# A hybrid decoder block on one core: where the rotated q/k projections stand among the plain ones, and who orders the second half of the projections

## The chip, the cores and the metric

The kernel runs on one core of a Trainium2 chip. The metric is the device time of one execution in microseconds, the median of the runs; lower is better. The engines are named as the profile names them: PE (TensorE matmuls) and PEld (its weight loads), DVE (VectorE), ACT (ScalarE), POOL (GpSimd) and SP (SyncE, which here only issues DMAs). Each engine works through its own instructions in a fixed order, and waits on semaphores where it needs another engine or a DMA.

## The reference, cut to what matters

One layer of a decoder block over 2048 positions of width 1024, all in float32:

```python
h = rms_norm(x, g_norm) * (1.0 + scale) + shift
proj = h @ w_in          # 1024 -> 8 x 1024
x_rnn, z_rnn, q, k, v, z_attn, g_r, g_a = split(proj)
# branch A: conv, gates, scan over x_rnn; times silu(z_rnn); @ w_out_rnn
# branch B: q and k get a partial rotary turn, then dilated attention
qh = apply_partial_rope(q.reshape(B, S, N_HEADS, HEAD_DIM), cos, sin)
kh = apply_partial_rope(k.reshape(B, S, N_HEADS, HEAD_DIM), cos, sin)
```

The rotary turn touches the first 32 of the 128 channels of each of the 8 heads: `x1*cos - x2*sin` and `x2*cos + x1*sin`, with `x1` and `x2` 16 channels each. The other 96 channels of q and k pass unturned. After the two branches come their output projections, sigmoid merge gates, one more projection and a final norm.

## The kernel before

**The stages.** Sequence positions are cut into four banks of 512 columns, and two banks make a half. For each half `f` in (0, 1) the kernel projects v first (`values_half`, which also builds the operands of the second bank), then the other seven blocks of `w_in` as 28 *pairs* (a pair is 256 output rows by the half's 1024 columns), and at the end comes a long stage that weaves attention with the output projections. In the trace the pairs of the first half run from about 150 to 752 us, those of the second from about 849 to 1445 us, and the last stage from there on.

**A pair** (`strassen`, L349) multiplies a 2x2 block of the weights with a 2x2 block of the activations by Winograd's scheme, in seven *products*. A product is 12 matmuls (four k-blocks, each float32 value as a high and a low part, three matmuls for a product of two such numbers). The products accumulate in the PSUM tiles X (two buffers), Z, W, V and Y (one each). ACT copies X to `u1`, DVE makes `u2` from Z and `u3` from W, and four *totals* leave a pair through `done(i, j, ps, u)`: after products V (1,1), X (0,0) and Y (1,0), and after the last product V (0,1), which is issued one product into the next pair (`last_product`, L409). So between the end of a pair's last V and the next pair's first V on the same PSUM tile there stand two products, Z and W; in that time DVE must have read the total.

**Who prepares the weight operands.** In the first half each product's weight operand `S` is made on the way: SP loads raw blocks `R` (256 KB, L254), DVE forms Winograd sums `s` (L285, L286, L294, L299), ACT rounds to the high part (L159), POOL subtracts for the low part (L165), and ACT's queue stores the result (512 KB, L277) to DRAM as `sD`. In the second half SP loads the finished `S` from `sD` (L318), seven tiles ahead, one each time a product is done with its tile. Instead, the second half prepares the output projections' weights (`output_weights`, L421): 32 blocks, every six products one, each a load `R` (L430) at product 6x+1, one ACT and one POOL operation at 6x+4 into the single-buffered tiles `s1` and `s2`, and two 256 KB stores `wD` (L440) at 6x+6.

**The order.** A counter `n_prod` counts products. `steps_after` and `later` put a step after a given product: when that product has been traced, `run_late` (L219) traces the steps that are due. Within `tc.manual_schedule()` each engine gets its instructions in the order in which the program traces them. Outside it, the framework's scheduler orders them with the help of a simulated time line, and may pull a later instruction ahead. Before the change the first half's pairs stand in such a block (L1202 to L1204), and the second half's don't.

**The pairs of a half** (`pair_order`, L1057, and the loop at L1206): 22 pairs (recurrent, gate and two plain q ones) from the pool `rp`, then the *tail* of six pairs from the pool `qp`: q rotated, k rotated, and four plain ones (q, k, k, k). A rotated pair (L996) holds the 32 turned channels of all 8 heads. Each of its totals takes a tile `t0`; q is scaled by ACT first (L988 or L993); then a step `shuffle` (DVE stream shuffle into `t1`, L1007, and POOL's `t0*Ct`, L1008), and one product later a step `add` (DVE's `t1*St`, L1012, and `t1+t0`, L1013) with four stores. `t0` has 4 buffers in the first half and 5 in the second, `t1` has 3. A plain pair (L1034) has the totals, for q the scaling, and stores.

**What else is in the tails.** In the first half's tail `next_norm` (L1147) loads the next bank of x (two loads of 1 MB on SP at once, L501), squares it on ACT with row sums (L1154, steps 5 to 8), takes the inverse root (steps 9 and 10) and scales it on DVE (L1158, steps 11, 13, 15, 17). During the last pair `next_even` (L1163) turns it on PE (L521) and builds eight operand parts (`build`, L524: ACT L531, DVE `hf` L538, then DVE L168 or POOL L165). In the second half's tail `residual_gate` (L1113) loads eight 512 KB blocks `gw` and adds them up on DVE (L1126, L1128), one every third product.

Of the kernel before, what the change touches and what calls it, by code (L numbers as in the profile page):

```python
# [10 lines left out]
F32 = mybir.dt.float32  # L11
# [9 lines left out]
P = 128  # L21
S = 2048
D = 1024
# [66 lines left out]
def decoder_block(ctx, tc, x, c, positions, g_norm, w_mod, b_mod, w_in, b_gate, conv_w, conv_b,  # L90
# [422 lines left out]
    n_built = [0]  # L513

# [8 lines left out]

    def build(st, names, xs, k, first=False, keep=None, pt=None):  # L524

        hh, hl = B[names[k // KH]]
        if pt is None:
            pt = turned(xs, k)
        pv = pt[:].rearrange("p r j -> p (r j)")
        g, s = gs[:, k : k + 1], sh[:, k : k + 1]  # L530
        nc.scalar.activation(hh[:, k % KH, :], pv, AF.Identity, bias=s, scale=g)  # L531
        if keep is not None or first:
            hf = keep if keep is not None else T(st, [P, CH], F32, "hf", bufs=2)[:]
            last_copy[0] = nc.scalar.activation(hf, pv, AF.Identity, bias=s, scale=g).ins
            last_lo[0] = lo_dve(hl[:, k % KH, :], hf, hh[:, k % KH, :])
        else:
            hf = T(st, [P, CH], F32, "hf", bufs=2)
            nc.vector.tensor_scalar(hf[:], pv, g, s, ALU.mult, ALU.add)  # L538
            (lo_dve if k % 3 == 0 else lo_pool)(hl[:, k % KH, :], hf[:], hh[:, k % KH, :])
# [442 lines left out]
    NT0, NT1 = (4, 5), 3  # L982
# [13 lines left out]
    def rotated_pairs(qp, f, Ct, St):  # L996

        for base, dstT, qs in QK:
            def rotated(i, j, ps, u, dstT=dstT, qs=qs):
                n = 2 * f + j  # L1000
                cq = slice(j * CH, (j + 1) * CH)
                t0 = T(qp, [P, CH], F32, "t0", bufs=NT0[f])
                wait, v = scaled(t0, ps, u, qs), []

# [4 lines left out]

                def add():  # L1010
                    t1 = v[0]
                    nc.vector.tensor_tensor(t1[:], t1[:], St[:, cq], ALU.mult)  # L1012
                    nc.vector.tensor_tensor(t1[:], t1[:], t0[:], ALU.add)  # L1013
# [40 lines left out]
    others = [1, 2, 2, 1, 2, 2, 1, 3]  # L1054
    is_plain = lambda n: n % 6 == 3

    def pair_order():  # L1057
# [89 lines left out]
    def next_norm():  # L1147

        xs = load_x(xp, 2, "x", 2)
        ss = T(xp, [P, 3, 4], F32, "ss")  # L1150

        def square(r):
            jk = T(xp, [P, D], BF16, "hf", bufs=2)
            nc.scalar.activation(jk[:], xs[r], AF.Square, accum_out=ss[:, 0, r : r + 1])  # L1154

        for r in range(4):
            later(5 + r, lambda r=r: square(r))
            later(11 + 2 * r, lambda r=r: nc.vector.tensor_scalar(xs[r], xs[r], ss[:, 1, r : r + 1], None, ALU.mult))  # L1158
        later(9, lambda: rstd_first(ss))
        later(10, lambda: rstd_last(ss))  # L1160
# [22 lines left out]
    for f in range(2):  # L1183
# [18 lines left out]
        if f == 0:  # L1202

            order.enter_context(tc.manual_schedule())  # L1204
# [11 lines left out]
        plain_at[0] = lambda: T(qp, [P, CH], F32, "t0", bufs=NT0[f])  # L1216

        touch = [T(qp, [P, CH], F32, tag, bufs=n) for tag, n in (("t0", NT0[f]), ("t1", NT1), ("u1", 1), ("u2", 2), ("u3", 1))]
# [584 lines left out]
```

## Time and profile before

| what | value |
|---|---|
| median of the runs | 2324.31 us (2319.95 to 2330.45) |
| span of the profiled execution, first to last instruction | 2322.0 us |
| median less that span | 2.3 us |
| PE busy | 2233.7 us (96%), 11459 matmuls |
| DVE, ACT, POOL busy | 1347.5, 1238.5, 971.1 us |
| moved by DMA | 573.41 MB, 247 GB/s over the span |

The profile gives the profiled execution's span and no time of its own beside it; what lies around the span is taken as the 2.3 us between it and the median. Three views are used below. The table by stage has, for each stretch of time, its length, then the busy time of PE, PEld, DVE, ACT and POOL with the number of instructions in brackets, the share of full TensorE clock that was granted, the mean busy share of the DMA engines, and GB/s. The table of waits has who waited for whom: microseconds in total, times, the longest. The timeline has start, duration, engine, line, operation, output<-input, and in square brackets how long the engine had been idle and what ended that. In the groups of instructions the number after the bar is busy time, then the mean ns of one, then idle time before them. Matmul ends are modelled, so starts are the better guide on PE.

### The profile page before, as it was taken

The numbers are of one execution on the slowest core, as the hardware profiler recorded it, in microseconds if no ns is written. First come the engines' busy times: TensorE is split into PE (matmuls) and PEld (weight loads), VectorE is DVE, ScalarE is ACT, GpSimd is POOL, SyncE is SP. The second block draws the span as 40 slices with busy tenths as digits, with TensorE's granted clock in tenths as the row PEclk, the third lists the DMA queues.
The fourth block names the chain that finished last, engine by engine and source line by source line (L and its number), as shares of the span: only waits on it lengthen the run. The fifth ranks groups of instructions, "written<-read, shape, count | busy, mean of one in ns | idle before, by whom it ended". The sixth has DMA issues, their size and how long they took to land.

```text
span 2322.0 us, 34101 instructions
## 1 busy us (share of the span) xinstructions
PE 2233.7 (96%) x11459; PEld 1868.9 (80%) x11461; DVE 1347.5 (58%) x2424; ACT 1238.5 (53%) x2412; POOL 971.1 (42%) x734
## 2 busy tenths in 40 slices
PE   8999999999979998999999999999989898989998
PEld 4998788888858997877888877888879797868887
DVE  4828787768483706344444362367666777667343
ACT  4737667668433625555546311567768777534211
POOL 1457576766465333323111020446565655433100
PEclk9999999999989999999999999999999999999999
DMA  7367787887989487998776897979988888798532
GB/s 262 105 216 246 248 290 252 291 282 256 295 253 299 125 266 269 318 312 283 247 227 201 280 290 234 294 245 270 274 252 253 240 249 243 232 313 276 170 123 95
DMA packets 429013, 573.41 MB, mean 247 GB/s; under 512 B 72135, under 2 KB 293027, under 8 KB 427813
## 3 DMA queue, kind: packets, MB, share of 16 engines
q1 hardware_dynamic: 390996, 451.47, 63.3%
q10 hardware_dynamic: 37648, 119.70, 13.3%
q8 instruction: 91, 1.49, 0.3%
q14 instruction: 86, 0.70, 0.1%
q0 software_dynamic: 192, 0.05, 0.0%
HBM read 357.18 MB, written 213.91 MB: 246 GB/s over the span
## 4 chain that ended last, share of the span: by engine, by line
PE 50%; DMA 9%; DVE 4%; ACT 3%; issue 2%; POOL 1%; SPq 1%; ACTq 0%; DVEq 0%; POOLq 0%
PE pj L151 11%; PE pq L151 8%; PE X L151 7%; PE V L151 7%; PE o L151 3%; PE Y L151 3%; PE sc L151 3%; PE Z L151 3%; PE W L151 3%; DMA R<-yaT 1%; DMA vraw<-vN 1%; DMA R<-oT 1%; PE pT L1419 1%; PE pg L151 1%; DMA wD<-s 1%
## 5 line engine op out<-in xcount | busy, mean ns | idle before, releaser
L151 PE MATMUL pj<-yh,S 128*128 128x512 f32 x1024 | 369.1, 405 | 5.5 <-DMA S<-wD 4.2
L151 PE MATMUL V<-T,S 128*128 128x512 f32 x1344 | 338.7, 401 | 22.6 <-DVE t L451 9.6
L151 PE MATMUL X<-T,S 128*128 128x512 f32 x1344 | 332.5, 396 | 3.9 <-ACT u L384 3.9
L165 POOL TENSOR_TENSOR S<-R,S 128x512 fp32r<-128x512 f32 x168 | 251.9, 1510 | 181.2 <-ACT S L159 66.0
L151 PEld LDWEIGHTS V<-T,S 128*128 128x128 f32 x1344 | 257.6, 193 | 86.5 <-ACT S L159 7.9
L151 PEld LDWEIGHTS X<-T,S 128*128 128x128 f32 x1344 | 253.8, 189 | 64.4 <-ACT u L384 4.4
L151 PEld LDWEIGHTS pj<-yh,S 128*128 128x128 f32 x1024 | 194.2, 190 | 42.8 <-DVE fg L1626 4.6
L151 PE MATMUL pj<-yl,S 128*128 128x512 f32 x512 | 202.0, 395 | 0.0
L1335 ACT ACTIVATE pp<-pp,st 128x256 f32<-128x256 f32 (+3 forms) x256 | 134.0, 524 | 107.1 <-DVE st L1334 106.3
L165 POOL TENSOR_TENSOR S<-s,S 128x512 fp32r<-128x512 f32 x84 | 129.0, 1536 | 136.4 <-ACT S L159 94.6
L151 PE MATMUL W<-T,S 128*128 128x512 f32 x672 | 167.2, 397 | 0.4 <-POOL S L165 0.4
L151 PE MATMUL Z<-T,S 128*128 128x512 f32 x672 | 165.7, 395 | 0.0
L151 PE MATMUL Y<-T,S 128*128 128x512 f32 x672 | 165.4, 395 | 0.0
L151 PEld LDWEIGHTS W<-T,S 128*128 128x128 f32 x672 | 126.9, 190 | 30.8 <-issue 0.9
L151 PEld LDWEIGHTS Y<-T,S 128*128 128x128 f32 x672 | 126.7, 189 | 29.5
L151 PEld LDWEIGHTS Z<-T,S 128*128 128x128 f32 x672 | 126.3, 188 | 29.3
L168 DVE TENSOR_TENSOR ptl<-pT,pth 128x384 fp32r<-128x384 f32 (+1 forms) x160 | 97.9, 629 | 64.6 <-ACT pth L159 62.3
L159 ACT ACTIVATE S<-R 128x512 fp32r<-128x512 f32 x168 | 102.1, 622 | 48.8 <-DMA R<-in_w_in_dram 17.7
L829 DVE SCALAR_TENSOR_TENSOR xc<-xr,par,xc 128x512 f32<-128x512 f32 x96 | 93.2, 971 | 57.6 <-ACT xc L823 56.0
L1399 ACT ACTIVATE pp<-pp,M 128x256 f32<-128x256 f32 (+3 forms) x256 | 118.0, 523 | 9.0 <-DVE M L1523 9.0
L1334 DVE CUSTOM_DVE_ANT_0 pp<-sc,msk 128x256 f32<-128x256 f32 (+3 forms) x256 | 105.1, 449 | 26.0 <-PE sc L151 23.4
L165 POOL TENSOR_TENSOR vh<-vraw,vh 128x256 fp32r<-128x256 f32 (+1 forms) x64 | 67.2, 1049 | 103.5 <-ACT vh L159 91.6
(327 smaller groups left out, 4708.9 us busy)
## 6 DMA issues: line engine op xcount, KB each, us to landing
sD<-S ACTq DMA_DIRECT2D x196, 512.0 KB, 4.0
S<-sD SPq DMA_DIRECT2D x196, 512.0 KB, 5.3
S<-wD SPq DMA_DIRECT2D x99, 512.0 KB, 5.5
R<-in_w_in_dram SPq DMA_DIRECT2D x136, 256.0 KB, 4.0
wD<-s ACTq DMA_DIRECT2D x64, 256.0 KB, 5.4
T<-in_w_mod_dram SPq DMA_DIRECT2D x8, 1024.0 KB, 12.0
vN<-ev SPq DMA_DIRECT2D x64, 128.0 KB, 2.8
zaT<-ev SPq DMA_DIRECT2D x32, 256.0 KB, 3.2
```

The costliest lines, as they stand in the source:

```text
L151: last_mm[0] = nc.tensor.matmul(o, lhsT=l, rhs=r, start=st, stop=sp, **kw).ins
L159: nc.scalar.activation(o, i, AF.Copy)
L165: nc.gpsimd.tensor_tensor(o, i, h.bitcast(F32), ALU.subtract)
L168: return nc.vector.tensor_tensor(o, i, h.bitcast(F32), ALU.subtract).ins
L829: nc.vector.scalar_tensor_tensor(xc, xr[:, i : i + CH], cw(i), xc, ALU.mult, ALU.add)
L1334: nc.vector.tensor_tensor_reduce(pdst, s_ps, mask, 1.0, 3e38, ALU.add, ALU.min, m_)
L1335: nc.scalar.activation(pdst, pdst, AF.Exp, bias=m_, scale=-1.0, accum_out=l_)
L1399: nc.scalar.activation(pp, pp, AF.Copy, scale=w)
L1419: nc.tensor.transpose(pt[:, c0 + j * P : c0 + (j + 1) * P], pp[i][:, k * P : (k + 1) * P], ident)
```

## The change

- `TAIL_ROTATED = (0, 1, 0, 1, 0, 0)`: the tail's order is now plain q, rotated q, plain k, rotated k, plain k, plain k, in both halves; `rotated_pairs` becomes a generator to be taken one at a time.
- A rotated total goes in three steps instead of two, each one product after the one before: shuffle (with POOL's product), turn (DVE's `t1*St`), add (DVE's sum, and the stores). The second total of a pair starts a product later than it did, and the third and fourth two products later.
- `t0` has 5 buffers in both halves. For the first half's tail pool `xp`, `hf` has one buffer instead of two.
- `next_norm` issues its two loads of x after products 3 and 10, squares at 16, 18, 20 and 22, takes the root at 23 and 25 and scales at 26, 28, 30 and 32.
- The second half's pairs stand in `tc.manual_schedule()` as well.

```diff
+    def n_hf(st):
+        return 1 if st is xp else 2
 ...
-            hf = T(st, [P, CH], F32, "hf", bufs=2)
+            hf = T(st, [P, CH], F32, "hf", bufs=n_hf(st))
 ...
-    NT0, NT1 = (4, 5), 3
+    NT0, NT1 = 5, 3
 ...
                 wait, v = scaled(t0, ps, u, qs), []
+                wait += (0, 1, 2, 2)[made[0]]
+                made[0] += 1
 ...
+                def turn():
+                    nc.vector.tensor_tensor(v[0][:], v[0][:], St[:, cq], ALU.mult)
+
                 def add():
                     t1 = v[0]
-                    nc.vector.tensor_tensor(t1[:], t1[:], St[:, cq], ALU.mult)
                     nc.vector.tensor_tensor(t1[:], t1[:], t0[:], ALU.add)
 ...
-                steps_after(n_prod[0], ((wait, shuffle), (wait + 1, add)))
+                steps_after(n_prod[0], ((wait, shuffle), (wait + 1, turn), (wait + 2, add)))
 
             strassen(qp, f, (base, "rotated"), rotated)
+            yield
 ...
+    TAIL_ROTATED = (0, 1, 0, 1, 0, 0)
 ...
-        for base, _, _ in QK:
-            yield (base, "rotated"), [wcol(base + hh * P, 32) for hh in range(H)]
-        for key in plain:
-            yield key, plain_pieces(*key)
+        rotated = iter(QK)
+        for r in TAIL_ROTATED:
+            if r:
+                base = next(rotated)[0]
+                yield (base, "rotated"), [wcol(base + hh * P, 32) for hh in range(H)]
+            else:
+                key = next(plain)
+                yield key, plain_pieces(*key)
 ...
-        xs = load_x(xp, 2, "x", 2)
+        xs = []
         ss = T(xp, [P, 3, 4], F32, "ss")
 
+        def load(r):
+            t = T(xp, [P, 2, D], F32, "x", bufs=2)
+            nc.sync.dma_start(t[:], xv[2, r : r + 2].rearrange("r j d -> j r d"))
+            xs.extend((t[:, 0, :], t[:, 1, :]))
 ...
+        later(3, lambda: load(0))
+        later(10, lambda: load(2))
         for r in range(4):
-            later(5 + r, lambda r=r: square(r))
-            later(11 + 2 * r, lambda r=r: nc.vector.tensor_scalar(xs[r], xs[r], ss[:, 1, r : r + 1], None, ALU.mult))
-        later(9, lambda: rstd_first(ss))
-        later(10, lambda: rstd_last(ss))
+            later(16 + 2 * r, lambda r=r: square(r))
+            later(26 + 2 * r, lambda r=r: nc.vector.tensor_scalar(xs[r], xs[r], ss[:, 1, r : r + 1], None, ALU.mult))
+        later(23, lambda: rstd_first(ss))
+        later(25, lambda: rstd_last(ss))
 ...
         order = ExitStack()
-        if f == 0:
-
-            order.enter_context(tc.manual_schedule())
+        order.enter_context(tc.manual_schedule())
 ...
-        rotated_pairs(qp, f, *tabs)
-        for n, _ in enumerate(plain, 3):
-            if n == 5 and f == 0:
+        rotated = rotated_pairs(qp, f, *tabs)
+        for n, r in enumerate(TAIL_ROTATED):
+            if n == len(TAIL_ROTATED) - 1 and f == 0:
                 next_even()
+            next(rotated if r else plain)
```

More of the change, by code (lines that the diff above doesn't have):

```diff
@@ L532, in build @@
         if keep is not None or first:
-            hf = keep if keep is not None else T(st, [P, CH], F32, "hf", bufs=2)[:]
+            hf = keep if keep is not None else T(st, [P, CH], F32, "hf", bufs=n_hf(st))[:]
             last_copy[0] = nc.scalar.activation(hf, pv, AF.Identity, bias=s, scale=g).ins
@@ L1215, in decoder_block @@
         plain_pool[0] = qp
[L1216 to L1218 removed]
+        plain_at[0] = lambda: T(qp, [P, CH], F32, "t0", bufs=NT0)
+        touch = [T(qp, [P, CH], F32, tag, bufs=n) for tag, n in (("t0", NT0), ("t1", NT1), ("u1", 1), ("u2", 2), ("u3", 1))]
         tabs = load_tables(qp, f)
```

8 lines of the change are left out of this document (5 added, 3 removed).

## The prediction

> **What bounds the kernel now.** I read the head of the page first, then a table by stage, then TensorE's waits in each stage, and for the long waits the timeline.
>
> ```profile
> span 2322.0 us, 34101 instructions
> PE 2233.7 (96%) x11459; PEld 1868.9 (80%) x11461; DVE 1347.5 (58%) x2424; ACT 1238.5 (53%) x2412; POOL 971.1 (42%) x734
> ```
>
> PE is busy 96% of the span. So an order of issue can win only what PE loses by waiting, and by the slower clock after a long wait. Cutting the trace where the stages begin shows where that is (columns: length, busy PE, PEld, DVE, ACT, POOL, clock, DMA share, GB/s):
>
> ```profile
> 150.60:609.40 458.80, 453.21 (x1950) 366.19 (x1949) 345.03 (x372) 316.83 (x505) 311.19 (x210) 1.00 0.78 267
> 609.40:750.00 140.60, 125.57 (x538) 100.88 (x538) 75.36 (x101) 45.71 (x81) 77.96 (x55) 0.94 0.88 281
> 849.40:1317.80 468.40, 457.12 (x1950) 368.35 (x1949) 211.74 (x285) 252.51 (x382) 108.52 (x85) 0.99 0.80 269
> 1317.80:1444.60 126.80, 124.29 (x521) 98.04 (x519) 53.92 (x73) 16.35 (x28) 16.89 (x12) 0.99 0.86 275
> ```
>
> These are the first half's 22 pairs, its tail, the second half's 22 pairs, and its tail. A product at full pace is this row of the chain:
>
> ```profile
> 682.23 2.79 PE X L151 x12
> ```
>
> 2.79/12 = 0.2325 us a matmul. The 22 pairs are 154 products and 96 gate matmuls, 1944 x 0.2325 = 452.0 us, with some 1.4 us of small transposes 453.4 us. The first half needs 458.8 for them and loses **5 to 6 us**; the second needs 468.4 and loses **15**. A tail's stretch holds 42 to 43 products, about 119 us, plus 2 to 3 us of transposes, first matmuls of the next stage or gate sums: the first tail loses **19 us**, the second **5**. Together about 45 us can be won in the stages that the change touches, and the rest of the span is not touched. The waits, first tail, then the second half's pairs, then its tail (total, times, longest):
>
> ```profile
> PE V L151 <- ACT S L159: 7.5, 1, 7.5
> PE V L151 <- DVE t L451: 7.2, 2, 7.0
> ...
> PE V L151 <- DVE ev L451: 3.8, 1, 3.8
> PE pg L948 <- DVE ev L943: 3.7, 1, 3.7
> PE pg L151 <- POOL xl L165: 2.9, 2, 1.4
> ...
> PE V L151 <- DVE t L451: 2.4, 1, 2.4
> ```
>
> So the first tail has two holes of 7 us, the second half a handful of small ones. The first hole in the timeline:
>
> ```profile
> 621.85 3.41 SPq L501 DMA_DIRECT2D x<-in_x_dram  x2
> ...
> 634.68 1.06 ACT L1154 ACTIVATE hf<-x 128x1024 bf16<-128x1024 f32 x1 [6.86 <-DMA sD<-S]
> ...
> 635.74 0.62 ACT L993 ACTIVATE t<-t 128x512 f32<-128x512 f32 x1
> ...
> 636.40 0.73 DVE L1007 STREAM_SHUFFLE t<-t 128x512 f32<-128x512 f32 x1
> ...
> 647.11 0.68 DVE L451 TENSOR_TENSOR t<-V,u 128x512 f32<-128x512 f32 x1
> ...
> 647.94 4.44 PE L151 MATMUL V<-T,S 128*128 128x512 f32 x12 [7.01 <-DVE t L451]
> ```
>
> Both loads of x are issued at 621.9, and land 12.8 us after issue:
>
> ```profile
> x<-in_x_dram SPq DMA_DIRECT2D x2, 1024.0 KB, 12.8
> ```
>
> 621.9 + 12.8 = 634.7, which is when ACT starts the first square after 6.9 us of idling (the row names a store; the landing fits better). Behind the square stands the scaling of q (L993), behind that DVE's shuffle, and behind the whole rotation the total that PE's V waits for. The second hole:
>
> ```profile
> 674.56 1.74 DVE L299 TENSOR_TENSOR s<-R,s 128x512 f32<-128x512 f32 x1
> ...
> 676.38 0.63 ACT L159 ACTIVATE S<-s 128x512 fp32r<-128x512 f32 x1 [10.14 <-DVE s L299]
> ...
> 677.05 5.18 PE L151 MATMUL V<-T,S 128*128 128x512 f32 x12 [7.50 <-ACT S L159]
> ```
>
> Here ACT waits 10.1 us for a Winograd sum, which stands in DVE's order behind rotations and scalings of x. DVE is simply late.
>
> **The change part by part.** *x in two parts, squares later.* The second load comes after product 10 and the first square after 16: 6 x 2.79 = 16.7 us, against a landing of 12.8 for both at once. SP's raw loads for the rotated pair no longer stand behind 2 MB. The first hole goes, 7.0 us and the slow product after it (4.3 instead of 2.79, from the starts 647.94 and 652.21): 8.5 us. If the cover fails, ACT stands as before, but in a plain pair.
>
> *Rotations apart, in three steps.* The groups of the first tail, and L1013 of the second tail, where POOL is nearly idle:
>
> ```profile
> L165 POOL TENSOR_TENSOR S<-R,S 128x512 fp32r<-128x512 f32 x29 | 41.3, 1431 | 20.3 <-ACT S L159 9.7 <-DMA R<-in_w_in_dram 7.5 <-issue 3.0
> L1012 DVE TENSOR_TENSOR t<-t,St 128x512 f32<-128x512 f32 x8 | 12.5, 1558 | 0.0
> L1013 DVE TENSOR_TENSOR t<-t,t 128x512 f32<-128x512 f32 x8 | 10.9, 1362 | 0.8
> L1158 DVE TENSOR_SCALAR x<-x,ss 128x1024 f32<-128x1024 f32 x4 | 4.2, 1038 | 0.0
> ...
> L1013 DVE TENSOR_TENSOR t<-t,t 128x512 f32<-128x512 f32 x8 | 5.4, 680 | 0.2
> ```
>
> With the shuffle's 0.73 (timeline above) a rotation costs DVE 1.56 + 1.36 + 0.73 = 3.65 us beside POOL's work. Two pairs in succession are 14 products, 39.1 us. Before, the two rotated pairs ask DVE for 8 rotations (29.2), 10 sums and totals from PSUM at 0.68 (6.8), 8 Winograd sums at no less (5.4) and four scalings of 1.04 (4.2): 45.6 us, **6.5 more than there is**, about the second hole. After, a rotated pair with the plain one behind it asks 14.6 + 6.8 + 5.4 = 26.8, with the x scalings 31.0, of 39.1. So the second hole goes too (7.5, and 5.02 - 2.79 = 2.2 for the slow product). POOL's 14 splits at 1.43 and four products fit as well (26 of 39.1). The third step itself adds nothing but waiting time for the tile, and the fifth `t0` covers it. What is late next is the start of the tail, where DVE idles for the gate stores of the pool before:
>
> ```profile
> 625.04 0.69 DVE L385 TENSOR_TENSOR u<-Z,u 128x512 f32<-128x512 f32 x1 [9.48 <-DMA gaT<-ev]
> ```
>
> A plain pair absorbs these 9.5 us: DVE has 9 x 0.68 = 6 us to do in its 19.5. Of 19 us I take **17**, since both holes lose their cause; bounds 8.5 (only the first hole) and 19.
>
> The Trainium skill ("SBUF — State Buffer", Who interferes with whom) says that a DVE instruction with two SBUF inputs and a GpSimd instruction reading SBUF exclude each other for a whole instruction. The trace goes part of the way: 0.68 alone, 1.36 to 1.56 beside POOL, not 0.68 + 1.3. Taken strictly, the rule lets me add both engines up: 18 POOL operations at 1.29 and 20 DVE ones at 0.69 make 37 of 39.1 us behind the rotated k, a margin of 2 us instead of 8. That speaks for the second rival below.
>
> *One `hf`.* DVE's next `hf` must wait for POOL's use of the last:
>
> ```profile
> L538 DVE TENSOR_SCALAR hf<-pg,gs,mod 128x512 f32<-128x512 f32 x6 | 4.8, 808 | 4.9 <-ACT T L531 4.9
> ...
> L165 POOL TENSOR_TENSOR T<-hf,T 128x512 fp32r<-128x512 f32 x3 | 3.9, 1294 | 4.2 <-DVE hf L538 4.2
> ```
>
> 0.81 + 1.29 = 2.1 us a build, in series. One build a product (2.79) hides that; the last three stand in a row and cost up to 3 x 0.81 = 2.4 us more, partly beside v matmuls that are ready. Queued behind the waiting `hf` are totals, which have two products to spare. I take **+1**; bounds 0, and 8 x 1.43 = 11 if every build waits for a split of the next stage's weights on POOL.
>
> *Second half, 22 pairs, program order.* The nearest evidence is the first half: the same pairs in the same order in such a block, 458.8 instead of 468.4 us, though DVE is busy 345 us there instead of 212, ACT 317 instead of 253 and POOL 311 instead of 109 (stage table). Its one long wait:
>
> ```profile
> PE X L151 <- ACT u L384: 3.9, 1, 3.9
> 263.28 1.28 ACT L936 ACT_TABLE_LOAD   x1
> ...
> 270.53 0.57 ACT L384 ACTIVATE u<-X 128x512 f32<-128x512 f32 x1
> ```
>
> That `u` stands behind table loads for the sines and, among others, three or four weight splits of 0.62 us, which the second half doesn't have. So the stage should come out between 458.8 (-9.6) and 453.4 (-15). I take the middle, **-12**. The output weights' steps move with it: the scheduler had pulled them to the front, into the busiest DMA stretch, with a quiet one behind it:
>
> ```profile
> 849.40:1105.00 255.60, 243.39 (x1022) 194.55 (x1021) 0.98 0.88 301
> 1105.00:1317.80 212.80, 212.41 (x914) 171.70 (x913) 1.00 0.71 230
> L440 ACTq DMA_DIRECT2D wD<-s x58: 326/326/627, 850.6 to 1076.8; - x58
> R<-in_w_out_attn_dram SPq DMA_DIRECT2D x16, 256.0 KB, 5.9
> ```
>
> 58 of the 64 stores stand before 1076.8; now they spread over 192 products. 32 x 768 KB = 25 MB over 595 us are 42 GB/s on top of 230: a share of 0.71 x 272/230 = 0.84 instead of 0.88 and 0.71. Tiles `S` are asked for 6 x 2.79 = 16.7 us ahead. SP now issues each of them after the product that frees its tile and before that product's stores, which costs a store no more than the product.
>
> *Second tail.* The same spreading of rotations removes the 2.4 us wait and its slow product, but weights traffic is added to a share of 0.86 (stage table): 0.86 x 317/275 = 0.99. I take **-2**, nearer to the first; bounds -4 and +8 (42 GB/s too much for 24 products, paid in full).
>
> *Into attention.* Two ordered blocks now follow each other; what lies between them (rounding `yh`, `yl`) is still free. **0**; bounds 0 and +6, were ACT's eight roundings to start behind the half's last total.
>
> Sum: 2322.0 - 17 + 1 - 12 - 2 = 2292 us span; with 2.3 us around it **2294.3 us** against the median of 2324.3. 0.5%, about what a measurement of this kernel can tell from no change, is 11.6 us: up to 2312.7 counts as faster.
>
> **The rivals.** *The second half gains nothing*: program order swaps the scheduler's holes for its own, because the output weights now sit among the recurrent steps to the end. For it: ACT and POOL wait on `wD` there already. Against: the first half with 7 more ACT operations a pair. 2322.0 - 17 + 1 + 2.3 = **2308**.
>
> *The rotated k stays too much for DVE and POOL*: its scalings of x (products 26 to 32) fall on its rotations, and the second hole remains. 2294.3 + 9.7 = **2304**.
>
> *Slower, by late output weights*: in program order ACT reaches the split of block x three products after SP issued its load, 8.4 us. If it lands later, ACT stands, and behind it `u`, the sigmoids, q's scaling; then DVE, then PE. The load takes 5.9 us now (row above), at a similar share. Before, ACT waited on these tiles too, and the stage lost 15 us:
>
> ```profile
> L159 ACT ACTIVATE s<-R 128x512 fp32r<-128x512 f32 x29 | 18.1, 626 | 36.8 <-DMA wD<-s 30.2 <-POOL s L165 3.1 <-DMA R<-in_w_out_rnn_dram 3.0
> ```
>
> 36.8 us of ACT's waiting with at most 15 us of PE's loss: 0.4 of it at worst. A landing of 13 us would be 32 x 4.6 = 147 us of waiting and 60 us lost: 2294 + 60 = **2354**. It decides from 30/0.4/32 = 2.3 us over 8.4, a landing of 10.7, on.
>
> **How the numbers follow.** Forecast 0.60, nothing from the second half 0.14, rotated k 0.12, late weights 0.14. The range takes in the first three: low end 2322 - 19 - 15 - 4 + 2.3 = 2286, less some us of scatter, 2281; high end 2308 with `hf` at its worse bound, 2318. Faster: 0.60 + 0.12 and somewhat under half of 0.14 (2308 is near the bound), 0.78; same 0.08; slower 0.14.
>
> **What would show it.** In the tail after: x landed before ACT's first square, no idling of ACT ahead of it, no wait of PE over 2 us; rotations at 3 us or more apart. In the second half: the 22 pairs in 455 to 459 us, `wD` stores out to the end of the tail, and a share near 0.84 in its middle. The forecast is wrong if PE waits for DVE or ACT in most second-half pairs, or if ACT's waits on `s` grow past 70 us.

## The result, and the profile after

| kernel | median | range | profiled execution | its span |
|---|---|---|---|---|
| before, in the same series | 2322.13 us | 2319.84 to 2330.45 | | 2322.0 us |
| after | 2298.52 us | 2293.75 to 2299.88 | 2299.88 us | 2298.1 us |

The ratio is **0.9889** (95% interval 0.9869 to 0.991): 1.1% faster, 4 us above the forecast of 2294.3. That the total came out near the forecast says little about its terms, as the stage table shows. The head of the page after:

```profile
span 2298.1 us, 34088 instructions
PE 2231.0 (97%) x11461; PEld 1867.5 (81%) x11461; DVE 1352.7 (59%) x2424; ACT 1239.5 (54%) x2412; POOL 974.6 (42%) x734
```

PE has the same work as before (2233.7 us busy then) in a span that is 24 us shorter. The table by stage, columns as before: the first half's 22 pairs, its tail, the projection of v, the second half's 22 pairs, its tail. A stage begins where its first product starts, and the tails end at the start of the last V.

```profile
150.56:609.35 458.79, 453.21 (x1951) 366.23 (x1949) 345.09 (x372) 316.78 (x505) 311.29 (x210) 1.00 0.77 268
609.35:743.42 134.07, 125.44 (x544) 100.97 (x543) 78.41 (x99) 46.33 (x81) 79.53 (x55) 0.97 0.94 290
743.42:840.26 96.84, 96.84 (x808) 96.27 (x807) 51.32 (x84) 47.29 (x84) 37.55 (x27) 1.00 0.47 142
840.26:1290.89 450.63, 450.63 (x1950) 365.36 (x1949) 209.11 (x285) 251.05 (x378) 105.50 (x81) 1.00 0.83 272
1290.89:1410.74 119.85, 119.81 (x509) 94.78 (x508) 48.69 (x72) 16.58 (x28) 22.44 (x16) 1.00 0.98 320
```

Of before, the stretch of v, and the second tail with its end cut in the same way (the others are in the prediction):

```profile
750.04:849.41 99.37, 97.95 (x813) 97.03 (x812) 47.26 (x82) 49.86 (x87) 42.44 (x30) 1.00 0.54 167
1317.82:1441.85 124.03, 121.52 (x509) 95.97 (x508) 53.23 (x72) 14.18 (x25) 14.14 (x10) 0.99 0.87 280
```

The account of the span is then: first tail 140.6 to 134.1, **-6.5**; v 99.4 to 96.8, **-2.5**; the second half's pairs 468.4 to 450.6, **-17.8**; second tail 124.0 to 119.9, **-4.2**; everything from there on 880.2 to 887.4, **+7.2**; the first pairs -0.1. The sum is -23.9. In the second half's pairs PE is now busy for the whole 450.63 us. TensorE's waits in the first tail, which before were 7.5 and 7.0 us at V:

```profile
PE V L151 <- DVE t L451: 3.5, 1, 3.5
PE X L151 <- ACT u L384: 2.0, 1, 2.0
PE X L151 <- ACT T L535: 1.9, 1, 1.9
PE pg L522 <- DVE hf L542: 1.3, 2, 0.9
```

In the text below, *loss* is worked out from the starts of PE's matmuls: time from one to the next beyond 0.2325 us (half of that for 256 columns), so that the slow matmuls after a wait are counted too. After, the first tail loses 2.2 us at 623, **6.5 at 661 to 671**, and 3.9 at 731 to 739. The middle one is new. PE, DVE, ACT and SP around it, from the timeline:

```profile
665.42 5.46 PE L151 MATMUL V<-T,S 128*128 128x512 f32 x12 [3.49 <-DVE t L451]
```

```profile
655.89 0.01 DVE L1015 LOAD_MASK_SELECT t<-t  x1 [5.64 <-ACT t L997]
...
659.55 1.77 DVE L1023 TENSOR_TENSOR t<-t,t 128x512 f32<-128x512 f32 x1 [0.50 <-POOL t L1016]
661.24 1.77 DVE L1019 TENSOR_TENSOR t<-t,St 128x512 f32<-128x512 f32 x1
662.92 1.75 DVE L299 TENSOR_TENSOR s<-R,s 128x512 f32<-128x512 f32 x1
664.60 0.68 DVE L451 TENSOR_TENSOR t<-V,u 128x512 f32<-128x512 f32 x1
```

```profile
646.48 0.35 ACTq L277 DMA_DIRECT2D sD<-S  x1
648.55 0.63 ACT L159 ACTIVATE S<-s 128x512 fp32r<-128x512 f32 x1 [5.30 <-DVE s L286]
654.85 0.33 ACTq L277 DMA_DIRECT2D sD<-S  x1
655.22 0.63 ACT L997 ACTIVATE t<-t 128x512 f32<-128x512 f32 x1 [6.04 <-DMA x<-in_x_dram]
```

```profile
646.48 0.59 SPq L1170 DMA_DIRECT2D x<-in_x_dram  x1
...
649.05 13.88 SPq L254 DMA_DIRECT2D R<-in_w_in_dram  x12
663.14 5.17 SPq L1026 DMA_DIRECT2D qT<-t  x6
```

Read from below: the second part of x (1 MB) is issued at 646.5, and behind it 12 loads of the rotated k's weights take SP 13.9 us to issue. In that time ACT stands for 6 us in front of the store of an operand (L277), which is in its own order ahead of the scaling of q (L997); the last store before it was 8.4 us earlier, and it goes out 0.1 us after x has landed (646.5 + 8.3 = 654.8). DVE's shuffle waits 5.6 us for that, then the rotation is bunched up ahead of the total (664.60) for which PE's V waits. The rows show the order of events; why the store waits for x is taken up under e9.

### The profile page after: what moved, and what is told of

Same layout as the page of the kernel before. It is cut to its first block, busy times and chain, and to the rows that moved or that the text cites. A ratio compares the mean times of both kernels' runs of the same rounds, so it can differ in the third digit from the quotient of the medians.

```text
span 2298.1 us, 34088 instructions
## 1 busy us (share of the span) xinstructions
PE 2231.0 (97%) x11461; PEld 1867.5 (81%) x11461; DVE 1352.7 (59%) x2424; ACT 1239.5 (54%) x2412; POOL 974.6 (42%) x734
## 4 chain that ended last, share of the span: by engine, by line
PE 53%; DMA 10%; DVE 3%; SPq 2%; issue 2%; POOL 2%; ACT 1%; ACTq 0%; POOLq 0%; DVEq 0%
PE pj L151 10%; PE X L151 8%; PE pq L151 8%; PE V L151 7%; PE Z L151 4%; PE W L151 4%; PE Y L151 3%; PE sc L151 3%; PE o L151 3%; DMA R<-in_w_in_dram 2%; DMA vraw<-vN 2%; DMA kT<-t 1%; PE pT L1441 1%; PE pg L151 1%; PE pT L1454 1%
## 5 line engine op out<-in xcount | busy, mean ns | idle before, releaser
L151 PE MATMUL V<-T,S 128*128 128x512 f32 x1344 | 333.4, 397 | 5.1 <-DVE t L451 3.5
L151 PEld LDWEIGHTS Y<-T,S 128*128 128x128 f32 x672 | 126.7, 189 | 29.5
L165 POOL TENSOR_TENSOR s<-R,s 128x512 fp32r<-128x512 f32 x32 | 44.1, 1378 | 245.7 <-ACT s L159 224.0
L159 ACT ACTIVATE S<-R 128x512 fp32r<-128x512 f32 x168 | 102.1, 622 | 50.8 <-DMA R<-in_w_in_dram 23.4
```

Source lines behind the costliest of these rows:

```text
L151: last_mm[0] = nc.tensor.matmul(o, lhsT=l, rhs=r, start=st, stop=sp, **kw).ins
L159: nc.scalar.activation(o, i, AF.Copy)
L165: nc.gpsimd.tensor_tensor(o, i, h.bitcast(F32), ALU.subtract)
```

## The experiments

All were timed against the kernel before on the same chip, so ratios are what to compare; the medians of before lay between 2318.8 and 2324.3 us. Stage times are from each run's profile, *attention* is the time from the start of the last V to the first exponential, *rest* that from the last V to the end of the span.

| run | median us | ratio (95%) | first tail | tail + v | pairs 2 | attention | rest |
|---|---|---|---|---|---|---|---|
| before | 2322.13 | 1 | 140.6 | 239.9 | 468.4 | 18.5 | 880.2 |
| after | 2298.52 | 0.9889 (0.9869-0.9910) | 134.1 | 230.9 | 450.6 | 23.4 | 887.4 |
| e1 order alone | 2306.10 | 0.9917 (0.9903-0.9932) | 140.3 | 239.7 | 450.6 | 21.1 | 885.5 |
| e2 order taken out | 2313.94 | 0.9948 (0.9933-0.9964) | 135.9 | 232.8 | 469.4 | 18.9 | 881.3 |
| e3 rotated first | 2294.10 | 0.9869 (0.9850-0.9887) | 136.9 | 232.6 | 450.5 | 19.5 | 882.1 |
| e4 x as before | 2294.58 | 0.9869 (0.9852-0.9885) | 127.8 | 230.6 | 452.1 | 21.3 | 878.7 |
| e5 second x later | 2295.16 | 0.9897 (0.9882-0.9912) | 132.5 | 230.6 | 450.6 | 22.0 | 884.3 |
| e6 long rows, other columns | 2287.43 | 0.9868 (0.9850-0.9886) | 123.0 | 222.1 | 450.6 | 22.5 | 885.4 |
| e7 two buffers | 2296.29 | 0.9905 (0.9889-0.9922) | 132.0 | 230.0 | 450.5 | 23.5 | 882.7 |
| e8 first outputs early | 2292.86 | 0.9887 (0.9872-0.9901) | 135.6 | 232.4 | 450.6 | 19.2 | 882.4 |
| e9 packed rows | 2288.74 | 0.9863 (0.9848-0.9877) | 123.5 | 222.7 | 450.5 | 23.5 | 886.0 |
| e10 two steps | 2299.78 | 0.9928 (0.9906-0.9951) | 138.1 | 236.5 | 450.7 | 20.8 | 883.2 |
| e11 before, long rows | 2318.56 | 0.9989 (0.9979-0.9999) | 134.3 | 233.8 | 469.2 | 18.8 | 884.6 |
| e12 packed and early | 2283.63 | 0.9829 (0.9816-0.9843) | 122.1 | 221.9 | 450.5 | 19.0 | 879.1 |

One thing to keep in mind: from the last V on, after, e1, e3 to e7, e9 and e10 run the same instructions, and their rest lies between 878.7 and 887.4 us. Between two single profiles, a difference of under some 9 us says nothing about this part.

### e1 and e2: the order of the second half, alone and taken out

e1 is the kernel before with this edit; e2 is the kernel after with it undone:

```diff
-        if f == 0:
-
-            order.enter_context(tc.manual_schedule())
+        order.enter_context(tc.manual_schedule())
```

> The kernel before, with one thing of the change: the second half's projection pairs in program order. Theory A (the two traces read side by side): the order alone shortens the second half's first 22 pairs from 468.4 to about 451 us (TensorE loses nothing there), and it costs about 5 us where attention begins, since the loads of the first output operand are no longer pulled ahead of the last pair; the first tail stays at 140.6 us; total about 2305 us (2302 to 2309). Theory B (the prediction's terms): the pairs take 456 to 459 us and nothing is lost at the start of attention; total about 2310. Theory C: the second half got shorter because the rest of the change left it in another state (buffers, SP's queue), so order alone gives less than 5 us: over 2317.

> The kernel after, with the second half's pairs left to the scheduler again; everything in the first tail stays changed. Theory A: first tail 134 us, values stage about 97 us, the second half's pairs back at about 468 us, the start of attention without its 5 us; total about 2313 (2310 to 2316). Theory B (the first tail is worth its 17 us as predicted, and something in the second half hid it): total 2305 to 2308. Theory C (the tail's edits did the second half's gain too): total below 2303.

Both came out by theory A: 2306.1 and 2313.9 us. The second half's 22 pairs of e1, beside 468.4 in e2 and before:

```profile
848.36:1299.00 450.64, 450.64 (x1951) 365.35 (x1950) 210.36 (x285) 250.88 (x378) 105.74 (x81) 1.00 0.83 272
```

So the order alone takes 17.8 us from this stage, to the tenth what the whole change takes. The product of the two ratios is 0.9917 x 0.9948 = 0.9865, and both together gave 0.9889; within the intervals, nothing speaks against the two parts being independent. Taken alone the order is worth 0.8%, the edits in the tail 0.5%.

### e3, e4 and e10: the three edits of the first tail, each undone

e3 takes back the order of the pairs, e4 the handling of x, e10 the three steps of the rotation; each leaves the other two in place:

```diff
-    TAIL_ROTATED = (0, 1, 0, 1, 0, 0)
+    TAIL_ROTATED = (1, 1, 0, 0, 0, 0)
```

> The kernel after, with the two rotated pairs again at the head of the tail (in both halves); rotation in three steps, x in two parts and one buffer for the interim tile stay. Theory A (the order of the pairs relieves VectorE, as the prediction had it): VectorE is overfull in the second pair again, the first tail loses 6 to 8 us: 140 to 142 us, the total 2304 to 2307. Theory B (the three-step rotation and the late x did all of it, the order of the pairs nothing): first tail 133 to 135 us, total 2297 to 2300. Theory C (the hole of 6.5 us that is left in the tail comes from the second part of x landing while the second rotated pair's weights load; with the rotated pair early these are apart): first tail 127 to 130 us, total about 2293.

```diff
-        later(3, lambda: load(0))
-        later(10, lambda: load(2))
+        load(0)
+        load(2)
         for r in range(4):
-            later(16 + 2 * r, lambda r=r: square(r))
+            later(5 + r, lambda r=r: square(r))
...
```

> The kernel after, with the next x loaded in one go at the head of the tail, squared and scaled at the steps of before. Theory A (ScalarE stands in order behind the first square until x has landed, and TensorE loses that time): the wait for x returns before the first square, 6 to 8 us lost early in the tail, while the later hole of 6.5 us shrinks because no x lands beside the second rotated pair's loads; first tail 133 to 140 us, total 2298 to 2305. Theory B (the load of x never held TensorE, the rotation did): no loss early in the tail; 127 to 130 us, total about 2293. The place of TensorE's losses tells them apart more than the total.

```diff
-                wait += (0, 1, 2, 2)[made[0]]
...
-                steps_after(n_prod[0], ((wait, shuffle), (wait + 1, turn), (wait + 2, add)))
+                steps_after(n_prod[0], ((wait, shuffle), (wait + 1, add)))
```

> The kernel after, with the rotation in two steps again at the delays of before; the order of the pairs, x in two parts and one buffer for the interim tile stay. Theory A (spreading the rotation over more products is what relieved VectorE in the tail): waits of TensorE for a total on VectorE of 3 us and more at both rotated pairs, the first tail 3 to 7 us longer (137 to 141), total 2301 to 2306. Theory B (the tail's gain came from taking the short weight loads apart from the load of x, whatever the rotation): first tail 132 to 136 us, total 2296 to 2300.

**e3**: 2294.1 us, tail and v 1.7 us longer, the total not longer (0.9869, with the interval of after overlapping). Theory A falls: behind the second rotated pair, where e1 with the same order loses 7.6 and 2.7 us, e3 loses 2.4, and another 2.8 thirty us later. Theory C had the total right and the tail wrong (136.9 instead of 127 to 130).

**e4**: x lands 11.1 us after issue, ACT waits 2.8 us for it in front of the first square, and PE loses nothing there:

```profile
630.40 1.06 ACT L1175 ACTIVATE hf<-x 128x1024 bf16<-128x1024 f32 x1 [2.82 <-DMA x<-in_x_dram]
```

With a plain pair at the head of the tail this wait had room. The hole of 6.5 us at 661 us shrinks to 1.7, so the tail itself is 6.2 us shorter than after; but v then loses 4.9 us waiting for POOL's splits of its weights, and tail and v together are 230.6 against 230.9. (One of these splits, at 774.13, takes 6.1 us where 1.3 is usual; what makes it long isn't shown.) Theory B in the tail, with the gain given back one stage later. So loading x in two parts brought nothing over the other edits.

**e10**: the hole of before returns, one pair later. PE, ACT and DVE:

```profile
713.24 3.33 PE L151 MATMUL V<-T,S 128*128 128x512 f32 x7 [8.10 <-ACT S L159]
```

```profile
712.58 0.63 ACT L159 ACTIVATE S<-s 128x512 fp32r<-128x512 f32 x1 [10.56 <-DVE s L299]
```

```profile
702.62 1.45 DVE L1179 TENSOR_SCALAR x<-x,ss 128x1024 f32<-128x1024 f32 x1
704.00 1.78 DVE L1020 TENSOR_TENSOR t<-t,St 128x512 f32<-128x512 f32 x1
705.88 0.69 DVE L1021 TENSOR_TENSOR t<-t,t 128x512 f32<-128x512 f32 x1
...
706.49 0.72 DVE L1015 STREAM_SHUFFLE t<-t 128x512 f32<-128x512 f32 x1
707.24 0.69 DVE L1020 TENSOR_TENSOR t<-t,St 128x512 f32<-128x512 f32 x1
709.09 1.74 DVE L1021 TENSOR_TENSOR t<-t,t 128x512 f32<-128x512 f32 x1 [1.15 <-POOL t L1016]
710.75 1.75 DVE L299 TENSOR_TENSOR s<-R,s 128x512 f32<-128x512 f32 x1
```

It is the same chain as the second hole of before: ACT waits over 10 us for the pair's last Winograd sum (L299), which stands in DVE's order behind a scaling of x, two rotations, and a wait of 1.2 us for POOL's half of one of them. The pairs are apart here, and the hole is as large as ever (8.3 us of loss, and 2.4 in the slow product behind it). Theory A, in the stage (+5.6 us in tail and v) and in the ratio (0.9928 against 0.9889, intervals that just touch); the total stayed under the 2301 that it gave. Of the three edits, the three steps (with the later starts that belong to them) are the one that removed the second hole. The other two, the place of the rotated pairs and the split of x, can each be taken back without making the kernel measurably slower (e3, e4).

### e5 and e6: what the new hole is made of

e5 issues the second part of x seven products later, with its squares and the scalings moved to fit; e6 reads the rotated pairs' weights as 256 adjacent columns in place of eight times 32, so that its q and k come from other columns than the reference's.

```diff
-        later(10, lambda: load(2))
+        later(17, lambda: load(2))
...
```

> The kernel after, with the second part of x loaded 7 products later (step 17 instead of 10, after the second rotated pair's weights), its two squares at steps 23 and 24 and the scalings one step later. Theory A (the hole of 6.5 us at 661 to 671 us comes from 1 MB of x landing beside the 28 small loads of the second rotated pair, which delays ScalarE's own stores and so the scaling of the interim tiles): the loss there falls to 2 us or less, tail and values together from 230.9 to about 225 us, total about 2293. Theory B (the hole belongs to the rotation on VectorE whatever lands): 4 to 6 us stay at 661 to 671 us, total 2297 to 2300. Theory C (the late x makes the building of the next operands late): the loss moves to 731 to 760 us and the total stays at 2298 or above.

```diff
-                yield (base, "rotated"), [wcol(base + hh * P, 32) for hh in range(H)]
+                yield (base, "rotated"), [wcol(base, 2 * P)]
```

> The kernel after, with the rotated pairs' weights read as 256 adjacent columns instead of eight times 32 (q and k then come from other columns of the weight, the work is the same): same bytes, 4 loads in place of 28 to 32, packets 4 times as long. Theory A (the small loads take SP and the DMA engines long, 13.9 us of issue in one row, and hold up what is queued behind them): the loss at 661 to 671 us falls below 2.5 us, tail and values together 225 to 227 us, total about 2293. Theory B (the 1 MB of x alone does it): the loss stays at 4 to 6 us, total 2297 to 2300.

In e5 nothing is lost at 661 to 671 us any more, so x was a part of it. But a new hole stands at 703 to 713 us (6.3 us of loss, V waiting 3.4 for ACT's split behind L299, as in e10): the scalings of x, now at 27 to 33, fall deeper into the rotations of k. Tail and v are 230.6, the ratio 0.9897: theory C in substance, though the loss went to 703 us and not to the place it named. In e6 all three late losses of the tail are gone; what is left is 2.1 us at 641. The first tail takes 123.0 us, 11 less than after:

```profile
608.10:731.12 123.02, 121.17 (x540) 98.36 (x538) 77.94 (x101) 45.20 (x78) 76.84 (x53) 1.00 0.96 306
PE X L151 <- ACT u L384: 1.9, 1, 1.9
```

Same bytes, same instructions on PE, DVE, ACT and POOL; only the loads of eight tiles differ. Their rows are 512 bytes long instead of 128, and there are 8 loads of 256 KB in place of 32 of 64 KB. No run changes one of these two without the other; *short loads* below means both. Theory A, and with more than it asked for: the loss at 731 us went too.

### e9 and e11: long rows in the kernel after and in the kernel before

e9 gives e6's long rows to the kernel after without changing what is computed: 16 transfers within DRAM, one every 8 products of the first half's pairs, collect the turned channels' columns.

```diff
+    rotD = scratch("rotD", [2, D, 2 * P])
...
+            for x in range(16):
+                b, hh = divmod(x, H)
+                after_prod.setdefault(n_prod[0] + 12 + 8 * x, []).append(lambda b=b, hh=hh: nc.sync.dma_start(
+                    rotD[b, :, hh * 32 : (hh + 1) * 32], wcol((2 + b) * D + hh * P, 32)))
...
-                yield (base, "rotated"), [wcol(base + hh * P, 32) for hh in range(H)]
+                yield (base, "rotated"), [rotD[base // D - 2]]
```

> The kernel after, with the rotated pairs' weights first copied within DRAM into 256 adjacent columns each, by 16 transfers of 128 KB, one every 8 products of the first half's pairs; the tail then loads them in long rows. The result is the reference's. Theory A (rows of 128 bytes in the tail hold up what is queued there; among the pairs there is room for them): tail and values together 222 to 225 us instead of 230.9, the first half's 22 pairs still 457 to 459 us; total 2288 to 2292, about 0.986 of before. Theory B (the short rows cost the same wherever they are read): the 22 pairs grow by 3 us or more, total 2295 or above.

Theory A: 2288.74 us (0.9863, an interval that overlaps that of after, so that the gain shows in the stages and not surely in the total), tail 123.5, tail and v 222.7, and the 22 pairs among which the copies run take 457.0 us (458.5 in e12, which has them too), no longer than after's 458.8. The transfers between 600 and 700 us, after and then in e9:

```profile
DMA packets 39590, 29.50 MB, mean 295 GB/s; under 512 B 27967, under 2 KB 34111, under 8 KB 39327
```

```profile
DMA packets 30333, 31.39 MB, mean 314 GB/s; under 512 B 14071, under 2 KB 24645, under 8 KB 30069
```

Half the short packets are gone, and the same 16 DMA engines, nearly full in both (shares 0.96 and 0.97 in these 100 us), carry 6% more. In e3 and e4, which keep the short loads, they carry 294 and 291 GB/s, in e6 and e12 316 and 319. The Trainium skill ("DMA: Bandwidth & Descriptors", Why small descriptors are slow) gives each packet a fixed overhead of about three cycles, at 32 bytes a cycle. By that a row of 128 bytes costs 7/4 of its bytes and one of 512 bytes 19/16, so the rotated pairs' 2 MB would cost as much as 1.1 MB less, 4% of 29.5: an estimate from that page, somewhat under the 6% of the trace.

SP and ACT's queue are held in e9 as well while x lands, but ACT for less long: its stores go out at most 3.7 us apart there, and the scaling of q (L999) doesn't wait for one.

```profile
641.34 0.34 SPq L1172 DMA_DIRECT2D x<-in_x_dram  x1
...
643.07 9.56 SPq L256 DMA_DIRECT2D R<-rotD  x3
```

```profile
646.05 0.33 ACTq L279 DMA_DIRECT2D sD<-S  x1
647.73 0.63 ACT L999 ACTIVATE t<-t 128x512 f32<-128x512 f32 x1 [1.12 <-DVE t L453]
...
649.58 0.33 ACTq L279 DMA_DIRECT2D sD<-S  x1
650.00 0.60 ACT L994 ACTIVATE t<-X 128x512 f32<-128x512 f32 x1 [1.12 <-DMA x<-in_x_dram]
```

What holds the store is a wait in the program. The trace gives for each DMA the semaphore that its landing raises, and between 600 and 700 us the DMAs of SP and ACT share eight of them, in after and in e9. Of the 951 DMAs of after for which the trace also tells when the one before on the same semaphore landed, none is issued earlier than that. The store at 654.85 has the semaphore of the x issued at 646.48, and goes out 0.08 us after x has landed, so the "DMA x<-in_x_dram" in ACT's row is meant literally, though the store has nothing to do with x. In e9 the store at 649.58 has the semaphore of x, and ACT stands for 1.1 us. In e5 the next DMA on the semaphore of the second x is a store of SP (676.62), and ACT isn't held by it.

So x didn't land faster with long rows: it takes 8.2 us in e9 and 8.3 in after. But SP issues it at 641.34 in e9 and at 646.48 in after, 5.1 us earlier, and ACT's wait is 4.9 us shorter. For the hole at 661 us, by these times, what the short loads cost is SP's time ahead of x. How much of the tail's other 4 us comes from the engines' lower rate, and how much from the number of loads, stays open.

e11 gives the long rows to the kernel before:

> The kernel before, with the rotated pairs' weights read as 256 adjacent columns (q and k then come from other columns, the work is the same); nothing of the change. Theory A (short rows stand behind both holes of 7 us in the first tail of before: x lands late, and what VectorE needs comes late): the first tail goes from 140.6 to 125 to 128 us and tail and values from 239.9 to 224 to 228; total 2308 to 2311. Theory B (only the first hole, the late x, comes from them; the second is the work of two rotated pairs on VectorE, as the prediction had it): first tail 131 to 134 us, total 2314 to 2316. Theory C (the short rows matter only to the kernel after): 140 us, total 2322.

As in e6, q and k come from other columns. Theory B in the tail: the first hole shrinks from 9 us of loss (7.0 and 2.0) to 4.1, the second stays. ACT's row there:

```profile
669.08 0.63 ACT L159 ACTIVATE S<-s 128x512 fp32r<-128x512 f32 x1 [10.15 <-DVE s L299]
```

In this run x is issued at 616.6 instead of 621.9 us, since SP gets through the rotated q's loads sooner, and the first square starts at 628.1 instead of 634.7. So the short loads were more than half of the first hole in before, and no part of the second. The total fell by 0.1% only (0.9989), less than B gave.

### e7: two buffers for the interim tile

To make room for the second buffer of `hf`, `t0` goes back from 5 buffers to 4.

```diff
-        return 1 if st is xp else 2
+        return 2
...
-    NT0, NT1 = 5, 3
+    NT0, NT1 = 4, 3
...
```

> The kernel after, with two buffers for the interim tile of the next operands as before, and 4 instead of 5 buffers of the rotated pairs' interim tile to pay for it. Theory A (the one buffer costs the 1.3 us that the transposes wait for VectorE there, as the prediction had it with 1): the loss at 731 to 739 us falls from 3.9 to 2.5 us, total 2297. Theory B (the one buffer lies behind the whole loss, ScalarE's late build too): the loss falls below 1 us, total 2294. Theory C (4 buffers are too few for the rotation): a new wait at 650 to 690 us, total 2300 or more.

The turns on PE wait 0.3 us for `hf` instead of 1.3, as theory A had it, but ACT's build (L535) now holds PE for 3.1 us instead of 1.9, and the place loses 5.3 us instead of 3.9. The ratio, 0.9905, doesn't differ from that of after. One buffer costs nothing that can be measured, as far as a run that also gives up a `t0` can tell.

### e8 and e12: the start of attention, and the best version

e8 issues the four row loads of the first output operand at products 172 to 181 of the second half instead of behind its last ones. For that the output weights' loads, which use the same buffers, go 5 products apart instead of 6.

```diff
-            if k < 4:
-                load_yd(yaT, 0, k)
...
-                after_prod.setdefault(n_prod[0] + 6 * x + d, []).append(fn)
+                after_prod.setdefault(n_prod[0] + 5 * x + d, []).append(fn)
+
+        for k in range(4):
+            after_prod.setdefault(n_prod[0] + 172 + 3 * k, []).append(lambda k=k: load_yd(yaT, 0, k))
```

> The kernel after, with the output weights' loads of the second half 5 products apart instead of 6, and the four row loads of the first output operand issued at products 172 to 181 of the half instead of after the last ones. Theory A (attention begins late because these loads come at the end of the ordered block): the first exponential starts 18.5 to 19.5 us after the last product's start, not 23.4 (21 in the other two runs with the order), total 2 to 4 us less, 2294 to 2297. Theory B (the other half of that operand, still loaded last, or the ordered roundings set the start): first exponential at 21 to 23 us, total 2298. Theory C (weights 5 products apart crowd the pairs): the second half's 22 pairs over 453 us.

After, ACT's roundings of this operand wait for those loads and end behind the last V (1410.74); then come q and k, and the first exponential:

```profile
1411.14 0.63 ACT L159 ACTIVATE yh<-R 128x512 fp32r<-128x512 f32 x1 [1.88 <-DMA R<-yaT]
1416.53 1.22 ACT L159 ACTIVATE yh<-R 128x512 fp32r<-128x512 f32 x2 [4.75 <-DMA R<-yaT]
...
1434.15 0.40 ACT L1357 ACTIVATE pp<-pp,st 128x128 f32<-128x128 f32 x1
```

In e8, where the last V starts at 1410.70 as well, they wait for nothing:

```profile
1408.60 2.19 ACT L159 ACTIVATE yh<-R 128x512 fp32r<-128x512 f32 x4
1410.68 2.19 ACT L159 ACTIVATE yh<-T 128x512 fp32r<-128x512 f32 x4
...
1429.86 0.40 ACT L1358 ACTIVATE pp<-pp,st 128x128 f32<-128x128 f32 x1
```

The first exponential comes 4.3 us sooner, theory A, and the pairs don't suffer. The total (0.9887 against 0.9889) doesn't show it. e12 puts e9 and e8 together:

> The kernel after with both of the edits that shortened a stage: the rotated pairs' weights copied into long rows among the first half's pairs, and the row loads of the first output operand issued early, with the output weights 5 products apart. The result is the reference's. Theory A (the two stages are independent and the time stays won): tail and values together 222 to 224 us, the first exponential 19 to 20 us after the last product's start, the rest 881 to 883 us; total 2283 to 2286, about 0.985 of before. Theory B (an earlier start of attention is given back within it, as 882.4 us of rest against 882.1 in a run without the edit suggests): rest 884 to 887 us, total 2287 to 2290, the same as with the long rows alone (0.9863).

2283.63 us, **0.9829** (0.9816 to 0.9843): theory A, and the fastest version that computes the reference's result, where after is at 0.9889 (0.9869 to 0.9910). The first tail and the DMA engines there:

```profile
607.55:729.66 122.11, 121.49 (x539) 98.44 (x538) 78.80 (x101) 45.35 (x78) 76.15 (x53) 1.00 0.96 309
```

Against e9 it gains 0.0034, 8 us, where the earlier start accounts for 4.5. The rest of it, and why e8 alone gained nothing in the total, stays open; the scatter of the last stage is of that size.

## Why the prediction was right, and where it was wrong

The total was right by luck: terms that were wrong cancelled. Against the forecast span of 2292, the first tail with the one buffer and v came out 7.0 us worse (-9.0 instead of -16), the second half's pairs 5.8 better, the second tail 2.2 better and the last stage 7.2 worse; with -0.1 that is the 6.1 us to 2298.1.

- **First tail, -17: the step that failed.** Both old holes did go, as the prediction had it, and without short loads the tail is worth the 17 (140.6 to 123.5 in e9, 122.1 in e12). What it left out is what the edit moved x next to. It took the split of x as pure relief ("SP's raw loads for the rotated pair no longer stand behind 2 MB"). But the second part, after product 10, is issued just ahead of the rotated k's loads (products 11 to 13), 12 of them in rows of 128 bytes. The first square was covered (x landed at 654.8, the square starts at 663.3); what stood was a store of ACT on the semaphore of x, for 6.0 us, and behind it the scaling of q, DVE's rotations and PE's V. e5 and e6 each remove one of the two ingredients and the hole at 661 goes; only e6 and e9 keep the time.
- **The reasons for the two old holes.** *First hole, the late x*: right, with more than half of it from the short loads (e11). Ahead of a plain pair PE loses nothing by it (e4), but ACT's wait is also shorter there, 2.8 us instead of 6.9. *Second hole, 45.6 us of work for DVE in 39.1*: wrong as an account. With the pairs apart the sum was 31.0, and in e10 the hole is back; with the pairs together, in e3, it doesn't come. By e10's rows, what decides is how much of the rotations and scalings stands in DVE's order ahead of L299.
- **One `hf`, +1**: too small to be told (e7).
- **Second half's pairs, -12**: right in cause (e1, e2), too small. The bound of -15 rested on a floor of 453.4 us, which counts 154 products. But the last of them is issued one product into the tail, so the stretch holds 153: 1932 matmuls at 0.2325 are 449.2 us, with the 1.4 of transposes 450.6. The stage took 450.63, the floor itself. By the same floor the first half loses 8 us and not 5 to 6, and none of that was there. That the `u` behind table loads would not recur was seen; with the slow matmuls behind it, it is 5.7 us of that loss.
- **Second tail, -2**: -4.2, the other bound. e1 and e2 reach 120.6 and 119.5 us each with one half of the change.
- **Into attention, 0**: the bound of +6 named the mechanism, and it happened: 18.5, 18.9 and 18.8 us to the first exponential in the runs without the order, 19.5 to 23.5 in the nine with it, 19.0 and 19.2 where the loads are early (e12, e8). By e3's 19.5 the cost is not the same in every run. The step overlooked that the four `R<-yaT` loads, which the scheduler had pulled ahead to 1048 to 1071 us, are now in the ordered block's last products. The other 2 us of the +7.2 lie within the scatter of the last stage.
- **The rivals.** *Late output weights*: no. They land in 3.7 to 6.6 us, against the 8.4 that they have and the 10.7 from which it would decide:

```profile
DMA to landing us min/median/max: 3.7/5.2/6.6
L159 ACT ACTIVATE s<-R 128x512 fp32r<-128x512 f32 x32 | 20.0, 624 | 61.6 <-DMA R<-in_w_out_attn_dram 49.3 <-DMA R<-in_w_out_rnn_dram 9.2 <-DMA S<-sD 3.1
```

  ACT waits 61.6 us in front of their splits and PE loses under 1 us in the 22 pairs and 2 in the tail: the 0.4 us of loss per us of ACT's waiting was no rate. *The second half gains nothing*: no. *Rotated k too much*: not in after, but e5 and e10 show how near it is.

## What to carry to other kernels

When a load is moved, list what its queue issues in the ten microseconds around it, with bytes per row and number of loads: 2 MB in 32 loads with rows of 128 bytes cost this tail 11 us that the same bytes in 8 loads with rows of 512 didn't, and were best collected early, where DMA has room. Look also at which later DMAs share its semaphore, because in this kernel the engine that issues one of them stands until the load has landed. In an engine's fixed order, don't add up its work over a stretch; find the one instruction that another engine needs (here a Winograd sum) and count only what stands ahead of it. Where a block of instructions is put into program order, look for the loads that the scheduler had pulled across its end.

## What the runs showed of the hardware

- With the short loads the DMA engines moved 291 to 295 GB/s (after, e3, e4), with the long ones 314 to 319 (e9, e6, e12), at shares of 0.96 to 0.99 (above). Read 128 KB at a time among the first half's pairs, at a share of 0.81, the same short rows cost nothing that can be measured.
- An engine that issues a DMA is held when the program makes that DMA wait: ACT stood 6.0 us in after until the x on whose semaphore its store was had landed, and all that followed in its order stood too.
- VectorE beside GpSimd: operations on two SBUF inputs of 128x512 take 0.69 us alone and up to 1.78 while POOL works, and POOL's go from 1.30 to 1.77 (e10's rows above, and POOL's below from the same run). Reads of PSUM stayed at 0.68. The prediction's 1.56 and 1.36 were means over both cases; in the bunched stretches, which are those that matter, it is 1.75.

```profile
702.22 1.30 POOL L1016 TENSOR_TENSOR t<-t,Ct 128x512 f32<-128x512 f32 x1 [1.31 <-DVE t L1015]
703.48 1.74 POOL L165 TENSOR_TENSOR S<-s,S 128x512 fp32r<-128x512 f32 x1
707.29 1.77 POOL L1016 TENSOR_TENSOR t<-t,Ct 128x512 f32<-128x512 f32 x1 [2.06 <-DVE t L1015]
```
